# One small load on another queue, and a second norm whose instructions are tied in a written order

## The chip, the cores and the metric

The kernel runs on one core of one Trainium2 chip. The metric is the device time of one launch in microseconds (us). The kernel before was run three times: median 1348.87 us, from 1348.59 to 1349.04.

A core has five engines with one instruction queue each. PE (TensorE) multiplies matrices and takes its stationary operand through a weight load (PEld in the views). DVE (VectorE), ACT (ScalarE) and POOL (GpSimd) work elementwise. SP (SyncE) here only issues DMAs. ACT and POOL can issue DMAs as well. The transfers themselves run on 16 DMA engines.

## The reference, cut to what matters

One layer of a decoder with two request groups, 256 prompt tokens and 8 x 4 sample tokens (288 columns in the kernel), and one conditioning vector for the prompt and eight for the samples:

```python
def block(x, c, st_pool, st_conv, st_ssm, st_ffn, pos0, lp):
    mod = (silu(c) @ lp['w_ada'] + lp['b_ada'])
    sh1, sc1, g1, sh2, sc2, g2 = [m[:, None] for m in jnp.split(mod, 6, axis=-1)]
    h = rmsnorm(x, lp['norm1']) * (1 + sc1) + sh1
    proj = h @ lp['w_in']
    ...
    mix = jnp.concatenate([pool_out, ssd_out], axis=-1) @ lp['w_out']
    x = x + g1 * mix
    h2 = rmsnorm(x, lp['norm2']) * (1 + sc2) + sh2
    ffn_out, new_ffn = conv_ffn(h2, st_ffn, lp['w_up'], lp['ffn_conv_w'], lp['ffn_conv_b'], lp['w_down'])
    x = x + g2 * ffn_out
    return x, new_pool, new_conv, new_ssm, new_ffn
```

Everything is float32. The model width is 2048, which is 16 tiles of 128 (`KT`); the gated MLP has 43 tiles of 128 (`FT`).

## The kernel before, in words

**Layout and products.** Features lie on the 128 partitions, the 288 tokens on the free axis. Each weight matrix is streamed once in chunks of up to 128 x 1024 floats (512 KB). A float32 product is made of three products of a shorter format: `split` (L293) writes the rounded weight `whi` on ACT (L289) and the remainder `wlo` on DVE (L291), the operand is split into `xhi` and `xlo` in the same way (L495, L496), and `mm3` (L301) issues the three matmuls whi·xhi, whi·xlo and wlo·xhi (L303, L304, L305).

**Slots.** `load` (L267) issues a DMA on SP's queue into a slot of a ring. The class `_W` keeps the rings. Ring `raw` and ring `rawa` hold raw chunks. During the two projections before the second norm four slots are in `rawa`; L1109 moves them to `raw`, so that from there on `raw` has 12 slots and `rawa` none. There are four slots each for `whi` and `wlo` then.

**Order.** A list scheduler orders the instructions of each engine by program order, priority and readiness in its own simulation. `tc.high_priority()` lets an instruction go ahead; `in_order(...)` (L210) ties the instructions written inside it to the written order on the named engines, and leaves other instructions free to come between.

**The start.** L185 loads the conditioning vectors (`ct`, 72 KB) from SP's queue, L544 loads x in four parts (`xa`, 576 KB each) behind it, then come the first conditioning weights. ACT waits for `ct`, takes its SiLU (L208), and then squares the first part of x (L970); DVE squares the second and fourth (L972). PE sums the squares (L974).

**The conditioning product.** The six parts of `mod` are each 16 steps of k. A step is two chunks (`adap`, part, k, half) and four matmuls that stand in four column groups of PE (8 records in the trace, since each is made in two passes). Parts 0 and 1 are made by `ada_group_units`, parts 2 and 3 by `ada_visits` (L405), two steps at a time out of ring `rawa`, parts 4 and 5 by `ada_part_units` (L444), one step per call. Part 5, the gate g2, isn't needed before the down projection, so its steps serve as filling work for PE.

**The second norm.** The last output projection tile ends in `residual` (L1169, DVE) and `squares` (L1183, ACT). `final_sum` (L1199) sums the squares over partitions with PE (`col_sums`, L238, line 241), takes the root (ACT, L247) and reciprocal (DVE, L248), spreads the result over the partitions with PE into PSUM (`pb`, L254), and copies it to SBUF (ACT, L261). `modulate_steps` (L474) then makes the operand of one or two tiles: a product with rstd (L478, DVE), scale and shift of the 256 prompt columns (L486, DVE), of the 32 sample columns (L491, L492, POOL), and the split (L495 ACT, L496 DVE). The tiles k = 0 and 1 read rstd straight from PSUM, the later ones from the copy. Around it stand part 5's first five steps: two written ahead of `final_sum` and three behind it (`GA = (2, 3)`).

**The up stage.** For k = 0 to 15 the chunk `upk` (384 KB: the k-th rows of six up-projection tiles) is split and multiplied into six PSUM tiles, 18 matmuls for each k (L1244 to L1249). Two of these chunks are split ahead of the norm (L1234). Then `up_pair` (L1256) makes a gate tile and a value tile for each j; from j = 3 on two more steps of part 5 follow each pair (L1341) until all 16 are done. The down projection runs in three groups, each behind the pairs of its group.

Of the kernel before, what the change touches and what calls it, by code (L numbers as in the profile page):

```python
# [12 lines left out]
F32 = mybir.dt.float32  # L13
# [5 lines left out]
P = 128  # L19
D = 2048  # L20
KT = D // P
# [32 lines left out]

RB1, RB2, RB3 = 1.0, 1.0, 1.0
TK = 4
GA = (2, 3)
XM = (0, 2, 5, 9)
SM0 = 10
YC = [(0, 1), (1, 1)] + [(m, 2) for m in range(2, KT, 2)]  # L60
# [5 lines left out]
FK = 3  # L66
# [98 lines left out]
def kernel(ctx: ExitStack, tc, ins, outs):  # L165
    nc = tc.nc
# [13 lines left out]
    def aux(name):  # L180
        return px.tile([P, 512], F32, tag="aux", name=name)


    ct = kp.tile([P, KT, NC9], F32, tag="asb", name="ct")
    nc.sync.dma_start(ct, ins["c"])  # L185
    early = kp.tile([P, NE], F32, name="early")
    vec = kp.tile([P, NV], F32, name="vec")
    ident = early[:, K_ID:K_ID + P]
# [45 lines left out]
    def new_operand(name):  # L234
        xhi[0] = [kp.tile([P, N], F32R, tag="xhi", name=f"{name}h{k}", bufs=KT) for k in range(KT)]
        xlo[0] = [kp.tile([P, N], F32R, tag="xlo", name=f"{name}l{k}", bufs=KT) for k in range(KT)]

    def col_sums(ps, src, rhs, first, last):  # L238

        for c, a in enumerate((0, P, N - P)):  # L240
            nc.tensor.matmul(ps[:, c:c + 1], src[:, a:a + P], rhs, start=first and c == 0, stop=last,
                             skip_group_check=True)
# [24 lines left out]
    def load(key, ring="raw"):  # L267
        off, cols = S.items[key]
        t = wp[0].tile([P, RAWC], F32, tag=ring, name="raw_" + "_".join(map(str, key)))
        nc.sync.dma_start(t[:, :cols], wflat[off:off + P * cols].rearrange("(p n) -> p n", p=P))  # L270
        return t
# [21 lines left out]
    def split(raw, a, n, name, urgent=True, pin=False):  # L293
        with tc.high_priority() if urgent else nullcontext():
            cast, (hi, lo, rest) = split_steps(raw, a, n, name)
        if pin:
            tc.keep_in_program_order(cast)
            tc.keep_in_program_order(rest)
        return hi, lo
# [23 lines left out]
    def project(key, nk, opnd=None, order=None):  # L323
        for ps in project_units(key, nk, opnd, order):
            pass
        return ps


    def ada_mm(ps, raw, k, c0, nb, js):
        for j in js:  # L330
            c = c0 + (j - js[0]) * nb
            nc.tensor.matmul(ps[32 * j:32 * j + 32, :nb], sc_c[:, k, :], raw[:, c:c + nb],  # L332
                             start=(k == 0), stop=(k == KT - 1), tile_position=(0, 32 * j))
# [68 lines left out]
            nc.vector.tensor_tensor(o, src, b.unsqueeze(3).to_broadcast([P, 2, nj // 2, NC9]), ALU.add)  # L402
        ada_scale(0, 1, early[:, V_N1:V_N1 + KT], k0, gk)

    def ada_visits(parts, step):  # L405

        plan = [(part, k0) for part in parts for k0 in range(0, KT, step)]
        ahead, end = [], None

        def chunks(v):  # L410
            part, k0 = plan[v]
            for k in range(k0, k0 + step):
                for h in range(2):
                    ahead.append((k, h, load(("adap", part, k, h), "rawa")))
            yield
            yield

        yield from chunks(0)
        for v, (part, k0) in enumerate(plan):
            if end:  # L420
                ada_end(*end)
                end = None
            if k0 == 0:
                ps = pa.tile([P, 512], F32, tag="ada", name=f"adap{part}")
            n = 0
            for k, h, raw in ahead[::-1]:
                for j in (2 * h, 2 * h + 1):
                    with tc.high_priority() if n else nullcontext():
                        i = nc.tensor.matmul(ps[32 * j:32 * j + 32, :], sc_c[:, k, :],
                                             raw[:, 512 * (j % 2):512 * (j % 2) + 512], start=k == step - 1,  # L430
                                             stop=k == KT - step, tile_position=(0, 32 * j))
                    tc.keep_in_program_order(i)
                    n += 1
            ahead.clear()
            if k0 + step == KT:
                end = part, ada_sb(ps, 512, f"p{part}")
            yield
            yield
            if v + 1 < len(plan):
                yield from chunks(v + 1)  # L440
        ada_end(*end)
        yield

    def ada_part_units(part, ay=1):  # L444
        ps = pa.tile([P, 512], F32, tag="ada", name=f"adap{part}")
        for k in range(KT):
            raws = [load(("adap", part, k, h)) for h in range(2)]
            for h in range(2):
                ada_mm(ps, raws[h], k, 0, 512, range(2 * h, 2 * h + 2))
            if k % ay == ay - 1:  # L450
                yield
        asb = ada_sb(ps, 512, f"p{part}")
        yield
        ada_end(part, asb)
        yield
# [14 lines left out]
    def modulate(*args):  # L470
        for _ in modulate_steps(*args):
            pass
# [246 lines left out]
    def drain(gen):  # L719
        for _ in gen:  # L720
            pass
# [477 lines left out]
    def final_sum(name, rname, keep=True):  # L1199
        ps = fsum.pop()  # L1200
        col_sums(ps, sq_last[0], ones[:, 0:1], False, True)
        return rstd_of(ps, D, rname, keep)
# [27 lines left out]
            drain(adas)  # L1230


    adag2 = ada_part_units(5)
    for k in range(2):  # L1234
        ready[("upk", k)] = split(load(("upk", k)), 0, 2 * FK * P, f"upk{k}")
    for _ in range(GA[0]):
        next(adag2)
    rstd2p, rstd2 = final_sum("ssum2", "rstd2")
    for _ in range(GA[1]):
        next(adag2)  # L1240
    new_operand("h2")
    up0 = [(pm.tile([P, 512], F32, tag="mm", name=f"mm_up{i}") if i < 3 else aux(f"mm_up{i}"))
           for i in range(2 * FK)]
    for k0, n in [(0, 1), (1, 1)] + [(k, 2) for k in range(2, KT, 2)]:  # L1244
        modulate(x[:, k0:k0 + n, :], rstd2 if k0 > 1 else rstd2p, 1, 3, k0, n, f"n{k0}")
        for k in range(k0, k0 + n):
            hi, lo = ready.pop(("upk", k), None) or split(load(("upk", k)), 0, 2 * FK * P, f"upk{k}")
            for i in range(2 * FK):
                mm3(up0[i][:, :N], hi, lo, i, xhi[0][k], xlo[0][k], k == 0, k == KT - 1)  # L1249

# [4 lines left out]

    def up_pair(j):  # L1256
        pg = up0[2 * j] if j < FK else project(("gate", j), KT)
        gb = ff.tile([P, NG], F32, tag="gb", name=f"gb{j}", bufs=2)
        gs = gb[:, 2 + NP:].rearrange("p (b l) -> p b l", b=NB)
        nc.gpsimd.memset(gb[:, 0:2], 0.0)  # L1260
        nc.gpsimd.tensor_copy(gs[:, :, 0:2], stf[:, j])
        nc.scalar.copy(gb[:, 2:2 + NP], pg[:, 0:NP])
        nc.scalar.copy(gs[:, :, 2:6], samp(pg[:, NP:N]))
        nc.gpsimd.tensor_copy(nff[:, j, 0:2], gb[:, NP:NP + 2])
        nc.gpsimd.tensor_copy(nff[:, j, 2:18].rearrange("p (b l) -> p b l", b=NB), gs[:, :, 4:6])
        fw = V_FW + 3 * j
        gc = ff.tile([P, NG], F32, tag="gc", name=f"gc{j}", bufs=2)
        nv = NG - 2
        nc.vector.tensor_scalar(gc[:, :nv], gb[:, 0:nv], vec[:, fw:fw + 1], vec[:, V_FB + j:V_FB + j + 1],
                                ALU.mult, ALU.add)  # L1270
        for i in (1, 2):
            nc.vector.scalar_tensor_tensor(out=gc[:, :nv], in0=gb[:, i:i + nv], scalar=vec[:, fw + i:fw + i + 1],
                                           in1=gc[:, :nv], op0=ALU.mult, op1=ALU.add)
        nc.scalar.activation(gc[:, :nv], gc[:, :nv], AF.Silu)
        pv = up0[2 * j + 1] if j < FK else project(("val", j), KT)
        act = ff.tile([P, N], F32, tag="act", name=f"act{j}", bufs=2)
        nc.vector.tensor_tensor(act[:, 0:NP], gc[:, 0:NP], pv[:, 0:NP], ALU.mult)
        gcs = gc[:, 2 + NP:].rearrange("p (b l) -> p b l", b=NB)[:, :, 0:NL]
        nc.vector.tensor_tensor(samp(act[:, NP:N]), gcs, samp(pv[:, NP:N]), ALU.mult)
        ah = ff.tile([P, N], F32R, tag="ah", name=f"ah{j}", bufs=17)  # L1280
        al = ff.tile([P, N], F32R, tag="al", name=f"al{j}", bufs=17)
        nc.scalar.copy(ah, act)  # L1282
        nc.vector.tensor_tensor(al, act, ah.bitcast(F32), ALU.subtract)
        acts[j] = (ah, al)
# [53 lines left out]
    for gi, (k0, nk) in enumerate(DGROUPS):  # L1338
        for j in range(k0, k0 + nk):
            up_pair(j)  # L1340
            if gi == 0 and j >= 3:  # L1341
                next(adag2, None)
                next(adag2, None)
            if j >= SM0:
                next(states, None)
            if gi and j == k0:
                drain(adag2)
                down(gi - 1)
# [170 lines left out]
```

## Time and profile before

| what | value |
|---|---|
| median of three runs | 1348.87 us |
| the profiled execution, its own time | 1348.87 us |
| its span (first to last instruction) | 1347.1 us |
| busy PE / DVE / ACT / POOL | 99% / 61% / 43% / 17% of the span |
| bytes moved | 323.19 MB, mean 240 GB/s |
| granted PE clock, mean | 0.997 |

The profiled execution took as long as the median of the runs, so a time read in its views can be set against the median as it is. What lies outside the span (1.8 us) is launch and end. In the timeline rows a line gives the start, the time from the first start to the last end of a merged run of equal instructions, engine, line, operation, tiles, shapes and count; square brackets give how long the engine sat idle before and what ended that. A matmul's record is longer than the time in which PE can take the next one: matmuls of 288 columns follow each other every 0.13 us, while each record lasts 0.29. A record names its tiles without numbers, so `raw_adap` is a chunk of any part.

### The profile page before, as it was taken

To read this page: it belongs to the slowest core of one execution; us is meant where nothing else is said; L and a number is where in the kernel's file an instruction comes from. 1 tells how busy PE (TensorE), PEld (TensorE's weight loads), DVE (VectorE), ACT (ScalarE), POOL (GpSimd) and SP (SyncE) were. 2 spreads that over 40 slices of the span, in tenths; PEclk is the share of its full clock that TensorE was granted. 3 is DMA by queue.
4 is the path that set the end of the run, shared out by engine and by line. 5 is a ranking of instruction groups with operands and counts; after the bars stand their busy time and mean duration, and the time that the engine had idled before them with its cause. 6 is when DMAs were issued, how large, how long until landed. Compare 5 with 4: busy or idle time off the path is not lost.

```text
span 1347.1 us, 26219 instructions
## 1 busy us (share of the span) xinstructions
PE 1330.4 (99%) x10517; PEld 1245.7 (92%) x10517; DVE 822.6 (61%) x1382; ACT 576.2 (43%) x909; POOL 224.0 (17%) x449
## 2 busy tenths in 40 slices
PE   9999999999999999999999999999999999999997
PEld 7889998786799889999999999999999999999997
DVE  5675569879755468555655545666655556566543
ACT  5343245676743335433443334443433334444442
POOL 0000012123122122110211001221210011122221
PEclk9999999999999999999999999999999999999998
DMA  9999678887798877787555556555555565566521
GB/s 372 405 408 368 230 286 305 305 330 294 253 398 333 333 299 233 267 280 247 181 184 185 164 174 190 195 192 195 180 165 169 188 195 186 188 197 197 178 78 71
DMA packets 97482, 323.19 MB, mean 240 GB/s; under 512 B 10768, under 2 KB 19920, under 8 KB 97360
## 3 DMA queue, kind: packets, MB, share of 16 engines
q1 hardware_dynamic: 93600, 310.79, 66.5%
q0 software_dynamic: 3184, 9.69, 2.0%
q8 instruction: 82, 1.34, 0.4%
q10 hardware_dynamic: 576, 1.03, 0.2%
q14 instruction: 40, 0.33, 0.1%
HBM read 309.78 MB, written 10.39 MB: 238 GB/s over the span
## 4 chain that ended last, share of the span: by engine, by line
PE 93%; DVE 2%; DMA 2%; ACT 1%; issue 1%; POOL 0%; SPq 0%; DVEq 0%; POOLq 0%; ACTq 0%
PE mm_down L304 7%; PE mm_down L303 7%; PE mm_down L305 7%; PE mm_gate L303 6%; PE mm_val L304 6%; PE mm_gate L304 6%; PE mm_gate L305 6%; PE mm_val L305 6%; PE mm_val L303 6%; PE xbc L303 5%; PE xbc L304 4%; PE xbc L305 4%; PE adag L378 2%; PE adap L332 2%; PE mm_out L303 2%; PE mm_out L304 2%
## 5 line engine op out<-in xcount | busy, mean ns | idle before, releaser
L304 PE MATMUL mm_down<-al,whi_down 128*128 128x288 f32 x688 | 202.5, 294 | 0.0
L303 PE MATMUL mm_down<-ah,whi_down 128*128 128x288 f32 x688 | 202.4, 294 | 0.0
L305 PE MATMUL mm_down<-ah,wlo_down 128*128 128x288 f32 x688 | 202.0, 294 | 0.0
L304 PE MATMUL mm_val<-h2l,whi_val 128*128 128x288 f32 x640 | 189.1, 296 | 0.0
L304 PE MATMUL mm_gate<-h2l,whi_gate 128*128 128x288 f32 x640 | 189.1, 295 | 0.0
L303 PE MATMUL mm_gate<-h2h,whi_gate 128*128 128x288 f32 x640 | 188.8, 295 | 0.0
L305 PE MATMUL mm_val<-h2h,wlo_val 128*128 128x288 f32 x640 | 188.4, 294 | 0.0
L305 PE MATMUL mm_gate<-h2h,wlo_gate 128*128 128x288 f32 x640 | 188.4, 294 | 0.0
L303 PE MATMUL mm_val<-h2h,whi_val 128*128 128x288 f32 x640 | 187.9, 294 | 0.0
L291 DVE TENSOR_TENSOR wlo_gate<-raw_gate,whi_gate 128x1024 fp32r<-128x1024 f32 x80 | 98.4, 1229 | 136.5 <-ACT whi_gate L289 136.5
L291 DVE TENSOR_TENSOR wlo_down<-raw_down,whi_down 128x1024 fp32r<-128x1024 f32 x96 | 108.0, 1125 | 116.7 <-ACT whi_down L289 116.7
L289 ACT CAST whi_down<-raw_down 128x1024 fp32r<-128x1024 f32 x96 | 92.4, 962 | 167.2 <-PE mm_down L304 119.2
L289 ACT CAST whi_gate<-raw_gate 128x1024 fp32r<-128x1024 f32 x80 | 84.1, 1051 | 159.7 <-PE mm_gate L304 77.9
L289 ACT CAST whi_val<-raw_val 128x1024 fp32r<-128x1024 f32 x80 | 84.1, 1051 | 127.4 <-issue 111.3
L303 PE MATMUL xbc<-h1h,whi_xbc 128*128 128x288 f32 x448 | 133.4, 301 | 0.8 <-ACT h1h L495 0.7
L304 PE MATMUL xbc<-h1l,whi_xbc 128*128 128x288 f32 x448 | 132.0, 296 | 0.0
L305 PE MATMUL xbc<-h1h,wlo_xbc 128*128 128x288 f32 x448 | 130.3, 296 | 0.0
L303 PEld LDWEIGHTS mm_down<-ah,whi_down 128*128 128x128 f32 x688 | 129.2, 188 | 0.0
L304 PEld LDWEIGHTS mm_down<-al,whi_down 128*128 128x128 f32 x688 | 129.1, 188 | 0.0
L305 PEld LDWEIGHTS mm_down<-ah,wlo_down 128*128 128x128 f32 x688 | 129.0, 187 | 0.0
L303 PEld LDWEIGHTS mm_gate<-h2h,whi_gate 128*128 128x128 f32 x640 | 120.3, 188 | 5.0 <-ACT ah L1282 3.4
L305 PEld LDWEIGHTS mm_gate<-h2h,wlo_gate 128*128 128x128 f32 x640 | 120.5, 188 | 0.0
(334 smaller groups left out, 2978.2 us busy)
## 6 DMA issues: line engine op xcount, KB each, us to landing
raw_adap<-wflat SPq DMA_DIRECT2D x128, 512.0 KB, 5.9
raw_gate<-wflat SPq DMA_DIRECT2D x80, 512.0 KB, 3.7
raw_val<-wflat SPq DMA_DIRECT2D x80, 512.0 KB, 3.5
raw_ada<-wflat SPq DMA_DIRECT2D x64, 512.0 KB, 9.6
raw_xbc<-wflat SPq DMA_DIRECT2D x50, 512.0 KB, 9.1
raw_down<-wflat SPq DMA_DIRECT2D x48, 512.0 KB, 3.5
raw_out<-wflat SPq DMA_DIRECT2D x32, 512.0 KB, 7.3
raw_down<-wflat SPq DMA_DIRECT2D x32, 384.0 KB, 3.5
```

Of the source, the lines that this page charges most:

```text
L289: yield nc.scalar.copy(hi[:, :n], raw[:, a:a + n])
L291: yield hi, lo, nc.vector.tensor_tensor(lo[:, :n], raw[:, a:a + n], hi[:, :n].bitcast(F32), ALU.subtract)
L303: nc.tensor.matmul(ps, whi[:, w], bh, start=first, stop=False)
L304: nc.tensor.matmul(ps, whi[:, w], bl, start=False, stop=False)
L305: nc.tensor.matmul(ps, wlo[:, w], bh, start=False, stop=last)
L332: nc.tensor.matmul(ps[32 * j:32 * j + 32, :nb], sc_c[:, k, :], raw[:, c:c + nb], start=(k == 0), stop=(k == KT - 1), tile_position=(0, 32 ...
L378: i = nc.tensor.matmul(ps[32 * j:32 * j + 32, :nb], sc_c[:, ck, :], raw[:, c:c + nb], start=q0 + n == 0, stop=q0 + AQ[gi] >= nq and n + 1 ...
```

## The change

It has three parts.

1. `ct` is loaded by a DMA issued on ACT's queue; x is then the first load on SP's.
2. The second norm is written inside one `in_order` block for PE, ACT and DVE: step 0 of part 5, the column sums, the root, step 1 of part 5 between the reciprocal and the spreading matmuls (`mid`), then steps 2 and 3. Behind them stand the modulation of tiles 0 and 1, interleaved; tile 0's sample columns are made on DVE and not on POOL. The copy of rstd from PSUM (`later=True`) is written behind the reads of tiles 0 and 1 from PSUM. The split of `upk` 2 stands at the end of the block, and the split of `upk` 3 loses its high priority; it and the later ones stand behind the modulation of their tile. Four steps of part 5 are in the block, not five.
3. The other twelve steps of part 5 are made by `ada_visits`, in visits of two steps out of ring `rawa`: four slots go from `raw` to `rawa` behind the norm and stay there, so `raw` has 8 slots for the rest of the kernel. From pair 3 on, a visit's four loads are written between the gate tile and the value tile and its matmuls behind the pair. `ada_visits` takes a PSUM tile that already holds the first steps (`ps`, `begun`).

```diff
-GA = (2, 3)
+GA = 4
...
-    nc.sync.dma_start(ct, ins["c"])
+    nc.scalar.dma_start(ct, ins["c"])
...
-    def ada_visits(parts, step):
+    def ada_visits(parts, step, ps=None, begun=0):
 
-        plan = [(part, k0) for part in parts for k0 in range(0, KT, step)]
+        plan = [(part, k0) for part in parts for k0 in range(begun, KT, step)]
...
-                                             raw[:, 512 * (j % 2):512 * (j % 2) + 512], start=k == step - 1,
+                                             raw[:, 512 * (j % 2):512 * (j % 2) + 512],
+                                             start=not begun and k == step - 1,
...
-    adag2 = ada_part_units(5)
     for k in range(2):
         ready[("upk", k)] = split(load(("upk", k)), 0, 2 * FK * P, f"upk{k}")
-    for _ in range(GA[0]):
-        next(adag2)
-    rstd2p, rstd2 = final_sum("ssum2", "rstd2")
-    for _ in range(GA[1]):
-        next(adag2)
+    fill = [[load(("adap", 5, k, h)) for h in range(2)] for k in range(GA)]
+    ps5 = pa.tile([P, 512], F32, tag="ada", name="adap5")
+
+    def fill_in(k):
+        for h in range(2):
+            ada_mm(ps5, fill[k][h], k, 0, 512, range(2 * h, 2 * h + 2))
+
     new_operand("h2")
+
+    def upk(k):
+        return split(load(("upk", k)), 0, 2 * FK * P, f"upk{k}", urgent=k > 3)
+
+    with in_order(nc.tensor.engine, nc.scalar.engine, nc.vector.engine):
+        fill_in(0)
+        ssum2 = fsum.pop()
+        col_sums(ssum2, sq_last[0], ones[:, 0:1], False, True)
+        rstd2p, rstd2 = rstd_of(ssum2, D, "rstd2", mid=lambda: fill_in(1), later=True)
+        for k in range(2, GA):
+            fill_in(k)
+        mod = [modulate_steps(x[:, k:k + 1, :], rstd2p, 1, 3, k, 1, f"n{k}", None if k else nc.vector)
+               for k in range(2)]
+        for k in (0, 0, 1, 0, 1):
+            next(mod[k], None)
+        rstd2 = rstd2()
+        drain(mod[1])
+        ready[("upk", 2)] = upk(2)
+    wp[0].move("rawa", "raw", "rawa")
+    adag2 = ada_visits((5,), AK, ps5, GA)
...
     for k0, n in [(0, 1), (1, 1)] + [(k, 2) for k in range(2, KT, 2)]:
-        modulate(x[:, k0:k0 + n, :], rstd2 if k0 > 1 else rstd2p, 1, 3, k0, n, f"n{k0}")
+        if n > 1:
+            modulate(x[:, k0:k0 + n, :], rstd2, 1, 3, k0, n, f"n{k0}")
         for k in range(k0, k0 + n):
-            hi, lo = ready.pop(("upk", k), None) or split(load(("upk", k)), 0, 2 * FK * P, f"upk{k}")
+            hi, lo = ready.pop(("upk", k), None) or upk(k)
...
         pg = up0[2 * j] if j < FK else project(("gate", j), KT)
+        if j >= FK:
+            next(adag2, None)
+            next(adag2, None)
...
-            if gi == 0 and j >= 3:
+            if FK <= j:
                 next(adag2, None)
                 next(adag2, None)
```

## The prediction

> **What bounds the kernel now.** I read the page first, its busy part; then PE's waits over the whole run; then the timeline of the three places that the change touches: the start, the second norm (484 to 500 us), the up stage.
>
> ```profile
> PE 1330.4 (99%) x10517; PEld 1245.7 (92%) x10517; DVE 822.6 (61%) x1382; ACT 576.2 (43%) x909; POOL 224.0 (17%) x449
> PE adap L429 <- DMA raw_adap<-wflat: 1.1, 1, 1.1
> PE mm_up L304 <- DVE h2l L496: 0.4, 1, 0.4
> PE mm_up L303 <- ACT h2h L495: 0.4, 1, 0.4
> ```
>
> PE is busy for 99% of the span, so whatever the change brings can only come out of the few places where PE waits or is filled with work that stands there to hide a wait. The last three rows (us in total, times, longest) say how little waits openly: at the second norm 0.8 us. The rest of the norm's latency is covered by steps of part 5, which PE has to do somewhere anyway. Hidden latency is worth nothing, and a filling step taken out has to be paid where it goes.
>
> **Part 1, the start.**
>
> ```profile
> 0.74 0.39 SPq L185 DMA_DIRECT2D ct<-c  x1
> 1.19 2.12 SPq L544 DMA_DIRECT2D xa<-x  x4
> ...
> 5.79 1.15 ACT L970 ACTIVATE sq<-xa 128x1152 f32<-128x1152 f32 x1
> 8.62 1.16 ACT L970 ACTIVATE sq<-xa 128x1152 f32<-128x1152 f32 x1 [1.68 <-DMA xa<-x]
> 10.09 1.36 DVE L972 TENSOR_TENSOR sq<-xa 128x1152 f32<-128x1152 f32 x1 [1.62 <-DMA xa<-x]
> 15.15 0.38 PEld L378 LDWEIGHTS adag<-raw_ada,sc_c 128*32 128x32 f32 x16 [0.24 <-DMA raw_ada<-wflat]
> ...
> 4.00:5.00 1.00, 1.00 (x6) 1.00 (x6) 0.00 (x0) 0.97 (x3) 0.00 (x0) 1.00 1.00 406
> ```
>
> The squares of the later parts of x start when their DMA lands, and the last conditioning chunk is waited for too. The last row is a stretch of the windows view (DMA share 1.00, 406 GB/s): from 4 us on the DMA engines are full. So the start runs at the pace of the transfers behind x's first issue. That issue moves from 1.19 to 0.74: **0.45 us** earlier, for all that follows, if nothing else is in the way. In the way can be `ct` itself. Today it goes ahead of x in one queue; then it shares the DMA engines with x's first part. In the worst case it lands only when that part does: 576 KB at 406 GB/s are 1.45 us later. ACT would then square the first part that much later; but before its second square it sits idle for 1.68 us, 1.23 when x comes 0.45 earlier, so 0.22 of the 1.45 is left over. PE's sums, which stand in a row behind these squares, may add a few tenths. Bounds -0.45 and +0.2; I take -0.35, near the first, since `ct` has only an eighth of one part's bytes. Nothing else waits on ACT's queue there: its first work needs `ct`.
>
> The Trainium skill (DMA: Bandwidth & Descriptors, Queues, rings and completion order) says that each DMA engine goes round robin between the queues it has work for, a whole packet at a time; another section of that page adds that a second issuing engine saves only issue time. That speaks for the delay of `ct`; with the worst case above the term would be about -0.2 in place of -0.35. No row of before has two queues competing at the start.
>
> **Part 2, the second norm.**
>
> ```profile
> 488.44 1.92 PE L332 MATMUL adap<-raw_adap,sc_c 128*32 128x512 f32 x16
> 489.12 0.54 ACT L1186 ACTIVATE sqa<-x 128x256 f32<-128x256 f32 x2 [6.13 <-DVE rs L1173]
> 490.29 0.83 PE L241 MATMUL ssum<-ones,sqa 128*128 128x1 f32 x6
> 491.16 0.26 ACT L247 ACTIVATE r3rstd<-ssum,epst 128x3 f32<-128x3 f32 x1 [1.50 <-PE ssum L241]
> 491.45 0.18 DVE L248 RECIPROCAL r3rstd<-r3rstd 128x3 f32<-128x3 f32 x1 [2.10 <-ACT r3rstd L247]
> 492.03 0.85 PE L254 MATMUL pbrstd<-early,r3rstd 128*128 128x128 f32 x6
> 492.81 2.77 PE L332 MATMUL adap<-raw_adap,sc_c 128*32 128x512 f32 x22
> 492.92 0.40 ACT L261 COPY rstd<-pbrstd 128x288 f32<-128x288 f32 x1 [1.50 <-PE pbrstd L254]
> 493.35 0.82 DVE L478 TENSOR_TENSOR h_n<-x,pbrstd 128x288 f32<-128x288 f32 x2 [1.72 <-ACT rstd L261]
> 494.09 0.95 DVE L291 TENSOR_TENSOR wlo_upk<-raw_upk,whi_upk 128x768 fp32r<-128x768 f32 x1
> 494.96 0.73 DVE L486 TENSOR_SCALAR h_n<-h_n,amul,ada 128x256 f32<-128x256 f32 x2
> 495.45 0.43 ACT L495 CAST h2h<-h_n 128x288 fp32r<-128x288 f32 x1 [0.67 <-DVE h_n L486]
> 495.94 1.06 PE L303 MATMUL mm_up<-h2h,whi_upk 128*128 128x288 f32 x6 [0.35 <-ACT h2h L495]
> 496.98 0.40 PE L304 MATMUL mm_up<-h2l,whi_upk 128*128 128x288 f32 x1
> 498.68 0.29 PE L303 MATMUL mm_up<-h2h,whi_upk 128*128 128x288 f32 x1
> ```
>
> The reader should see three detours. The squares end at 489.66 (489.12 + 0.54), but PE is still in two filling steps (16 records) until 490.29. DVE starts the product with rstd only when ACT's copy of the same PSUM tile ends (493.35, released by it). And a weight remainder (0.95) stands on DVE between that product and the scaling. After the change, step by step:
>
> - One step ahead of the sums: 488.44 to 489.44 (a single step takes 1.00, rows under part 3). The sums start when the squares are there, **489.7** and not 490.29; PE idles 0.26, since the tie lets no other step go ahead.
> - Sums to root 0.87 (490.29 to 491.16), root to reciprocal 0.29: the reciprocal ends at 491.05. On PE the sums take 0.76 until the next instruction, then one step of 1.00: 491.46. Here PE comes last, and the spreading starts at **491.5** and not 492.03.
> - From the spreading to DVE. The tail of the kernel has the same pair without a copy in between:
>
> ```profile
> 1336.88 0.85 PE L254 MATMUL pbrstdf<-early,r3rstdf 128*128 128x128 f32 x6
> ...
> 1337.77 5.92 DVE L1371 TENSOR_TENSOR x<-xf,pbrstdf 128x288 f32<-128x288 f32 x16 [0.95 <-PE pbrstdf L254]
> ```
>
> - That is 0.89, against 1.32 at the second norm: DVE starts at 492.4. Product 0.45, scaling 0.33 until the next, then the two sample instructions, which the first norm has on DVE already:
>
> ```profile
> 17.40 0.19 DVE L491 TENSOR_TENSOR h_g<-h_g,amul 128x32 f32<-128x32 f32 x1
> ...
> 17.63 0.19 DVE L492 TENSOR_TENSOR h_g<-h_g,ada 128x32 f32<-128x32 f32 x1
> ```
>
> - 0.23 and 0.19. The operand of tile 0 is ready for ACT at about 493.65, and PE follows the cast's start by 0.49 (495.45 to 495.94): **494.2**. PE's filling ends at the same time: 491.5 + 0.78 + 1.86 for two steps = 494.15. So filling and chain are balanced, and the gain here is 1.75.
> - The remainder of tile 0 (DVE, under half a us behind the cast) is there before PE has made its first six products, so the second wait (496.98) goes. Tile 1's products start 18 x 0.131 + 0.1 = 2.46 behind tile 0's, at 496.65, and not at 498.68: **-2.0** in all. Bounds: if POOL, which still makes tile 1's samples, or an untied instruction comes between, the second half of it is lost (-1.2); if the sums start with the first of the two squares, -2.3.
>
> What is late next is DVE at **tile 2**.
>
> ```profile
> 499.89 0.77 ACT L495 CAST h2h<-h_n 128x288 fp32r<-128x288 f32 x2 [0.26 <-POOL h_n L492]
> 501.12 0.93 DVE L496 TENSOR_TENSOR h2l<-h_n,h2h 128x288 fp32r<-128x288 f32 x2
> ```
>
> Today tile 2's remainder is ready at about 501.6, and PE wants it 0.8 behind 498.68 + 2.36, at 501.84: a margin of some 0.25. Then PE wants it 2.0 earlier, at 499.8. DVE begins 0.95 earlier, but has the 0.42 for the samples more, and the remainder of `upk` 2, which used to be made during the norm (one of the two at 494.09 and behind), now comes within this stretch; the one of `upk` 3 may follow tile 2. Added up from the rows above: products 0.82, scalings 0.73, samples 0.42, remainders of operands 0.93, `upk` 2 0.95, then for tiles 2 and 3 product 0.82, scalings 0.73 and one remainder 0.45: 5.85, so 498.25 without idling. That leaves 1.55 for what DVE waits for ACT and POOL. If the product for tiles 2 and 3 falls behind the `upk` 2 remainder, which itself waits for ACT's two casts, PE stands for about 1.2. Bounds 0 and +1.2; I take +0.2, near zero, since that product needs only the copy of rstd and DVE has a hole while it waits for tile 1's cast.
>
> **Part 3, the moved step and the visits.**
>
> ```profile
> 606.66 0.29 PE L305 MATMUL mm_val<-h2h,wlo_val 128*128 128x288 f32 x1
> 606.88 1.92 PE L332 MATMUL adap<-raw_adap,sc_c 128*32 128x512 f32 x16
> 608.74 0.40 PE L303 MATMUL mm_gate<-h2h,whi_gate 128*128 128x288 f32 x1
> ...
> 621.41 0.29 PE L305 MATMUL mm_val<-h2h,wlo_val 128*128 128x288 f32 x1
> 621.63 1.06 PE L332 MATMUL adap<-raw_adap,sc_c 128*32 128x512 f32 x8
> 622.63 0.40 PE L303 MATMUL mm_gate<-h2h,whi_gate 128*128 128x288 f32 x1
> ```
>
> Two steps behind a pair cost PE 1.86 (606.88 to 608.74), one step 1.00. Today eleven steps stand there, in five twos and a single; then twelve, in six twos. The number of switches between the two kinds of matmul stays six, so the fifth step costs 1.86 - 1.00 = **+0.86** (bounds 0.8 and 1.2).
>
> The loads are as many as before. A pair with a visit takes 14.75 us (606.66 to 621.41) and asks for 8 chunks, 4.2 MB: 284 GB/s, as today and under the 406 above. `raw` has 8 slots for the rest of the kernel, and PE eats one chunk in 3.15 us (24 matmuls), so they reach 25 us ahead. I cost this at 0; the cover is that lead. Upper bound 1.1, the wait that the first visit of parts 2 and 3 had (first fence); here the first visit's slots are free from the norm on.
>
> **The sum.** -0.35 - 2.0 + 0.2 + 0.86 = -1.3. Against 1348.87, both the profiled execution and the median: **1347.6 us**. With the bounds of its terms the forecast reaches from 1346.8 to 1348.4.
>
> **The rivals.**
>
> 1. Tile 2 starves PE (above): 1347.6 + 1.0 = **1348.6**. For it: the margin of 0.25 today, with two remainders made ahead. Against it: the hole on DVE. Chance 0.16.
> 2. The start gives nothing, because `ct` comes late beside x: 1347.6 + 0.35 = **1347.95**. Chance 0.10. Against it: the idle 1.68 on ACT.
> 3. **SP blocks, slower.** A visit's four loads need all four `rawa` slots, which come free only with the last matmul of the visit before. SP's queue is in order: chunks of the value tile written behind these loads would wait too.
>
> ```profile
> 207.55 1.75 SPq L270 DMA_DIRECT2D raw_adap<-wflat  x4
> 209.35 6.55 SPq L270 DMA_DIRECT2D raw_xbc<-wflat  x3
> ```
>
>    This is how the earlier visits look: four loads in a row, and another load right behind them. If the value chunk is the fifth, 2.6 MB have to move from the visit's end on, 6.5 us at 406 GB/s, behind 1.75 for issuing the four; then its cast, about 1 us. PE wants it after a gate tile, 6.3 us. That is 2.95 us in each of five pairs: 1347.6 + 14.8 = **1362.4**. It decides as soon as value chunks are issued less than about 9.3 us ahead. Against it: in those earlier visits, with fewer slots in `raw`, PE waited once, for 1.1. Chance 0.14.
> 4. The change doesn't do what it says: the list scheduler orders untied work anew, and the tied chain gains only the first 0.6 at the sums: -0.35 - 0.6 + 0.86, **1348.8**. Chance 0.09.
>
> **How the numbers follow.** The forecast has 0.51. About 0.2% (2.7 us) is what a measurement of this kernel tells from no change; forecast and rivals 1, 2 and 4 lie inside it. Slower by more is rival 3 and a remainder for an unforeseen wait in the up stage: 0.19. Faster by more needs 1.4 beyond the forecast, more than all the terms' ends give: 0.11. Within: 0.70. The range leaves out rival 3 and the tails: 1346.3 to 1349.7.
>
> **What would show it.** Right: first issue of x near 0.74 and the last square near 9.65; sums near 489.3 and first up matmul near 493.8 (the start's 0.35 taken off); the copy of rstd behind both products; twelve steps in six visits behind pairs 3 to 8. Wrong: PE waiting for h2h or h2l at tiles 2 to 4, for `raw_val` behind a visit, or a first square on ACT later than 7.0.

## The result, and the profile after

| kernel | median | from, to | runs |
|---|---|---|---|
| before | 1348.72 us | 1348.25, 1349.30 | 18 |
| after | 1351.16 us | 1350.14, 1352.07 | 18 |

The ratio is 1.0018, with an interval from 1.0011 to 1.0025. The changed kernel is 2.4 us slower: it lies above the range, and on the other side of no change than the forecast. The profiled execution of after took 1351.21 us, so its views can be set against the median.

The page's busy part of after:

```profile
PE 1331.6 (99%) x10517; PEld 1246.4 (92%) x10517; DVE 825.5 (61%) x1384; ACT 575.8 (43%) x909; POOL 221.3 (16%) x447
```

PE has the same 10517 instructions and is busy 1.2 us longer in a span that is 2.3 longer, so in sum about half of the loss is slower work and the other half waiting. DVE has the two sample instructions more, POOL two less.

Where it went is read first from landmarks. The tile views of after give, for each product, the first and the last start of a matmul (the two numbers ahead of the semicolon):

```profile
L303 PE MATMUL xbc<-h1h,whi_xbc x448: 289/294/402, 23.0 to 256.5; 128*128 128x288 f32 x150
L305 PE MATMUL mm_outp<-mixh,wlo_out x64: 289/294/297, 378.5 to 492.1; 128*128 128x288 f32 x64
L303 PE MATMUL mm_up<-h2h,whi_upk x96: 289/295/398, 497.9 to 536.2; 128*128 128x288 f32 x96
L303 PE MATMUL mm_gate<-h2h,whi_gate x640: 289/294/402, 536.6 to 1239.4; 128*128 128x288 f32 x160
L303 PE MATMUL mm_down<-ah,whi_down x688: 292/293/380, 715.1 to 1336.0; 128*128 128x288 f32 x172
```

Set against the same landmarks of before, in hundredths as the timelines of both have them:

| landmark | before | after | lag of after | gained or lost since the landmark above |
|---|---|---|---|---|
| first xbc matmul (end of the start) | 18.58 | 22.97 | +4.39 | +4.39 |
| last output projection matmul | 488.21 | 492.10 | +3.89 | -0.50 |
| first up matmul (end of the norm) | 495.94 | 497.88 | +1.94 | -1.95 |
| first gate matmul (end of the up stage) | 535.08 | 536.63 | +1.55 | -0.39 |
| last down matmul | 1333.62 | 1335.95 | +2.33 | +0.78 |

Everything behind the start is near the prediction's terms or better (-2.0 for the norm, +0.2 for tile 2, +0.86 for the moved step). The start costs 4.4 us where a gain of 0.35 was forecast. The timeline of after shows it:

```profile
0.74 0.41 ACTq L185 DMA_DIRECT2D ct<-c  x1
0.74 2.08 SPq L545 DMA_DIRECT2D xa<-x  x4
...
5.53 1.28 ACT L208 ACT_TABLE_LOAD   x1 [5.53 <-DMA ct<-c]
...
6.73 1.36 DVE L973 TENSOR_TENSOR sq<-xa 128x1152 f32<-128x1152 f32 x1 [5.02 <-DMA xa<-x]
6.82 0.34 ACT L208 ACTIVATE sc_c<-ct 128x144 f32<-128x144 f32 x1
7.18 1.28 ACT L965 ACT_TABLE_LOAD   x1
...
8.58 1.15 ACT L971 ACTIVATE sq<-xa 128x1152 f32<-128x1152 f32 x1
9.78 1.19 PE L975 MATMUL ssum<-sq,ones 128*32 128x288 f32 x8 [3.41 <-ACT sq L971]
...
12.05 1.19 PE L975 MATMUL ssum<-sq,ones 128*32 128x288 f32 x8
...
12.21 1.16 ACT L971 ACTIVATE sq<-xa 128x1152 f32<-128x1152 f32 x1 [2.48 <-issue]
14.44 1.36 DVE L973 TENSOR_TENSOR sq<-xa 128x1152 f32<-128x1152 f32 x1 [6.34 <-PE warm L229]
```

`ct` lands 4.7 us after its issue, as late as x's first part, and ACT stands until 5.53. Behind it come a table load, the SiLU of `ct`, another table load (L965, a dummy root), and only then the first square, at 8.58 and not at 5.79. PE, which sums the squares in order, waits 3.41 us for it. Then its sums take 1.19 us each. The windows view of after shows them at half the clock (columns: window, its length, busy time and records of PE, PEld, DVE, ACT, POOL, then the granted PE clock, DMA share, GB/s):

```profile
8.00:10.00 2.00, 0.22 (x4) 0.20 (x8) 0.09 (x1) 1.72 (x3) 0.00 (x0) 0.63 1.02 420
10.00:12.00 2.00, 2.00 (x12) 0.93 (x4) 0.00 (x0) 0.00 (x0) 0.00 (x0) 0.50 1.02 410
12.00:14.00 2.00, 2.00 (x13) 1.03 (x12) 0.00 (x0) 1.16 (x1) 0.00 (x0) 0.50 1.02 399
14.00:16.00 2.00, 2.00 (x14) 0.83 (x13) 1.36 (x1) 0.00 (x0) 0.00 (x0) 0.66 1.06 384
16.00:18.00 2.00, 2.00 (x31) 1.14 (x29) 0.46 (x1) 0.00 (x0) 0.00 (x0) 1.00 1.03 405
```

The granted clock falls to 0.50 while PE waits and is back only in the window from 14 us. Cut into quarters of a microsecond, the same view puts the fall at 8.53, 2.15 us after the last matmul record of PE has ended (6.38), and the rise at 15.36: 6.83 us, the last 5.6 of them with PE at work. While PE is slow, squares three and four (12.21 and 14.44) are late too: DVE's was released by PE's `warm` matmuls, which read the squares' buffer. The transfers aren't held up: 384 to 420 GB/s throughout.

The second norm in after's timeline:

```profile
492.33 1.07 PE L332 MATMUL adap<-raw_adap,sc_c 128*32 128x512 f32 x8
...
493.48 0.83 PE L241 MATMUL ssum<-ones,sqa 128*128 128x1 f32 x6
...
495.24 0.85 PE L254 MATMUL pbrstd<-early,r3rstd 128*128 128x128 f32 x6
...
496.13 0.45 DVE L479 TENSOR_TENSOR h_n<-x,pbrstd 128x288 f32<-128x288 f32 x1 [1.31 <-PE pbrstd L254]
...
497.81 0.40 ACT L260 COPY rstd<-pbrstd 128x288 f32<-128x288 f32 x1
...
497.88 0.66 PE L303 MATMUL mm_up<-h2h,whi_upk 128*128 128x288 f32 x3
498.41 0.40 PE L304 MATMUL mm_up<-h2l,whi_upk 128*128 128x288 f32 x1
```

Counted from the last output projection matmul (488.21 before, 492.10 after), the sums start at 1.38 (2.08 before), the spreading at 3.14 (3.82), DVE's first product at 4.03 (5.14) and the first up matmul at 5.78 (7.73). The copy of rstd stands behind both products, and no second wait follows.

### The profile page after: what moved, and what is told of

Read it like the earlier page. It is cut to its first block, busy times and chain, and to the rows that moved or that the text cites. A ratio compares the mean times of both kernels' runs of the same rounds, so it can differ in the third digit from the quotient of the medians.

```text
span 1349.4 us, 26215 instructions
## 1 busy us (share of the span) xinstructions
PE 1331.6 (99%) x10517; PEld 1246.4 (92%) x10517; DVE 825.5 (61%) x1384; ACT 575.8 (43%) x909; POOL 221.3 (16%) x447
## 4 chain that ended last, share of the span: by engine, by line
PE 94%; DVE 2%; ACT 1%; issue 1%; DMA 1%; POOL 0%; DVEq 0%; SPq 0%; POOLq 0%; ACTq 0%
PE mm_down L304 7%; PE mm_down L303 7%; PE mm_down L305 7%; PE mm_gate L303 6%; PE mm_val L304 6%; PE mm_gate L304 6%; PE mm_val L305 6%; PE mm_gate L305 6%; PE mm_val L303 6%; PE xbc L303 5%; PE xbc L304 4%; PE xbc L305 4%; PE adap L429 3%; PE adag L378 2%; PE mm_out L303 2%; PE mm_out L304 2%
```

## The experiments

Each kernel is told as a change to after, or to the run named.

**e1: only the queue of `ct` put back.** Theory A: the loss is all in `ct`'s place. The rival: the new norm and the visits cost something as well.

```diff
-    nc.scalar.dma_start(ct, ins["c"])
+    nc.sync.dma_start(ct, ins["c"])
```

> The changed kernel with the load of ct back on SP's queue ahead of x; all else as changed. Theory A (the loss sits in the start alone: the first xbc matmul moved from 18.57 to 22.96 us): the start falls back to 18.6, the norm and the visits keep what they gained, and the time is 1351.2 - 4.4 = 1346.8 us, at most 1347.4. Rival B (the later parts cost something that the trace hides): 1348.7 or more.

Measured: 1346.90 us, ratio to before 0.9988 (0.9979 to 0.9996). From e1's timeline:

```profile
0.75 0.38 SPq L185 DMA_DIRECT2D ct<-c  x1
...
1.18 2.01 SPq L545 DMA_DIRECT2D xa<-x  x4
...
2.61 1.28 ACT L208 ACT_TABLE_LOAD   x1 [2.61 <-DMA ct<-c]
...
5.66 1.15 ACT L971 ACTIVATE sq<-xa 128x1152 f32<-128x1152 f32 x1
...
6.85 1.36 DVE L973 TENSOR_TENSOR sq<-xa 128x1152 f32<-128x1152 f32 x1 [5.14 <-DMA xa<-x]
```

The first xbc matmul is at 18.3, and the norm's offsets are those of after (first up matmul at 5.78). One line takes 4.3 us out of the median (4.1 when after and e1 are each set against their own runs of before). So parts 2 and 3 of the change are worth -1.7 together, with an interval of the ratio that stays just below 1, and part 1 turns that into a loss.

**e2: before, with only `ct` on ACT's queue.** The same line of the diff, on its own.

> The kernel before with one edit: ct is loaded from ACT's queue. Theory A: ct lands near 5.4 us, ACT's first square starts near 8.6, PE sits idle for over 3 us and runs at a granted clock of 0.5 for some us; first xbc matmul near 23.0, time 1348.7 + 4.4 = 1353.1 us (1352.4 if the stretch before the output projection gives 0.6 back as it did in the changed kernel). Rival B: about 1348.7.

Measured: 1352.80 us, ratio 1.0030 (1.0018 to 1.0042); first xbc matmul at 22.3. `ct` releases ACT at 5.63, PE waits 2.94 for the first square, and the granted clock is 0.50 from 9.72 to 13.13 us, cut as finely as above. The line alone costs 4.2 us against before, as much as in the changed kernel.

**e3: PE kept busy until the square comes.** The loss can be ACT's lateness or PE's clock. More dummy matmuls ahead of the sums keep PE busy, and `ct` stays late.

```diff
-WU = (14, 2, 2, 2, 6)
+WU = (26, 2, 2, 2, 6)
```

> The changed kernel with 26 in place of 14 of the idle matmuls on ones that PE makes while it waits for the first square, so PE is busy until about 10.8 us. It parts the late ct from the clock. If the clock falls because PE sat idle: the granted clock stays at 1.0, the column sums of squares take 0.7 per group and not 1.2, the first xbc matmul comes at about 20.5, time about 1348.8 us (lateness alone costs some 1.9 of the 4.4). If the clock falls for another reason: clock 0.5 again and 1351.2 us.

Measured: 1349.62 us, ratio to before 1.0009 (1.0000 to 1.0018). From e3's timeline, and its windows view:

```profile
9.87 0.69 PE L975 MATMUL ssum<-sq,ones 128*32 128x288 f32 x8 [1.09 <-ACT sq L971]
```

```profile
10.00:12.00 2.00, 2.00 (x22) 0.95 (x19) 0.00 (x0) 0.71 (x1) 0.00 (x0) 1.00 1.02 408
```

The dummies end at 8.77, sooner than the 10.8 expected, so a wait is left: it shrinks to 1.09 us. The clock stays at 1.00, a sum takes 0.69 us and not 1.19. The first square is as late as in after (8.67), the first xbc matmul comes at 20.8. That splits the start: 20.8 - 18.3 (e1) = 2.5 us for lateness, 23.0 - 20.8 = 2.2 us for the clock. Of the 2.2 the median shows only 1.5 (1351.16 - 1349.62); e3's one wait for a conditioning chunk later on (`adap` at L429) was 1.6 us, against 0.8 in after.

**e6: ACT squares first.** `ct` stays on ACT's queue, but nothing ahead of the first square needs it any more: a dummy square on `epst` brings in the table early, the SiLU of `ct` follows the first square, and the dummy root the second.

```diff
-    nc.scalar.activation(sc_c[:, :, 0:NC9], ct, AF.Silu)
+    nc.scalar.activation(warm, epst, AF.Square)
...
-        nc.scalar.activation(warm, sc_c[:, 0, 0:1], AF.Sqrt, scale=0.0)
...
+                if q == 0:
+                    nc.scalar.activation(sc_c[:, :, 0:NC9], ct, AF.Silu)
+                else:
+                    nc.scalar.activation(warm, sc_c[:, 0, 0:1], AF.Sqrt, scale=0.0)
```

> The changed kernel, ct still on ACT's queue, but ACT squares the first part of x before it takes the SiLU of ct (a one-element square ahead brings its table in early; the root's table comes after the second square). If the only harm is that ACT waits for ct: the first square starts when x's first part lands (5.2 to 5.5), PE keeps its clock, the start is 0.45 earlier than with ct ahead of x, first xbc matmul at 18.1 to 18.6, time 1346.4 to 1346.9 us. If x's parts are slowed by ct's packets too: no better than the run with ct ahead of x on SP.

Measured: 1346.65 us, ratio 0.9984 (0.9975 to 0.9993): faster than before and after, and not to be told from e1. From e6's timeline:

```profile
0.74 2.02 SPq L545 DMA_DIRECT2D xa<-x  x4
...
5.33 1.16 ACT L970 ACTIVATE sq<-xa 128x1152 f32<-128x1152 f32 x1 [2.65 <-DMA xa<-x]
...
6.78 1.36 DVE L976 TENSOR_TENSOR sq<-xa 128x1152 f32<-128x1152 f32 x1 [5.07 <-DMA xa<-x]
```

Here x is first on SP, as the change wanted, and nothing stands in its way. It is issued at 0.74, which is 0.44 ahead of e1's 1.18, yet its second part is squared at 6.78 against 6.85: 0.07 earlier. That is one execution of each. In the five traces with `ct` ahead of x on SP (before, e1, and e8 to e10 below) this square starts between 6.85 and 7.11, so the gain is 0.07 to 0.33, and not all of the hoped 0.45.

**e4: x's first part as four transfers.** Why does 72 KB take as long as 576 KB? If the engines shared by bytes, `ct` would be through early. If they take turns row by row, it is through when as many rows of its neighbour are. Here the first part has four DMAs with rows of a quarter of the size.

```diff
-        nc.sync.dma_start(t, ins["x"][:, 4 * q:4 * q + 4, :])
+        for r in range(4 if q == 0 else 1):
+            r0, n = (r, 1) if q == 0 else (0, 4)
+            nc.sync.dma_start(t[:, r0:r0 + n, :], ins["x"][:, 4 * q + r0:4 * q + r0 + n, :])
```

> The changed kernel, but x's first part is loaded in four DMAs of one tile each (rows of 1152 bytes in place of 4608). It is run for the landing of ct alone (5.4 us in the changed kernel, 4.7 behind its issue); x comes later by the three more issues, so the time isn't compared. If the DMA engines take turns between the two queues row by row, ct's rows then stand behind rows a quarter as long: ct lands near 3.5 us. If they take turns in larger portions, or ACT's queue is slow by itself: 5 us or more.

Measured: `ct` lands 3.0 us after its issue, not 4.7. One run, 1348.77 us, too few to compare. The landing alone would also come out so if an engine finished its share of the whole first transfer, here a quarter as large, before it turned to `ct`; the packets below decide between the two.

**e5, e5b, e5c: `ct` on ACT's queue with nothing beside it.** Is ACT's queue slow in itself? x's first DMA is made to wait for the SiLU of `ct`, by a copy of one element into its buffer.

```diff
+        if q == 0:
+            nc.scalar.copy(t[:, 0, 0:1], sc_c[:, 0, 0:1])
```

> The changed kernel, but x's first DMA waits for ACT's SiLU of ct (ACT writes one element of that tile first), so ct travels alone on ACT's queue. Run for the landing of ct alone; the start is late by design. If ct was late only because x travels beside it: it lands near 2.6 us, as on SP's queue ahead of x. If ACT's queue is slow by itself: near 5.4.

This didn't isolate it: three conditioning chunks moved into the empty place on SP's queue, at 0.74, and `ct` landed in 3.8 us beside them. e5b made the first conditioning chunks and the `early` vectors wait too, of which the first:

```diff
+        if key[0] in ("ada", "xbc") and key[1] == 0:
+            nc.scalar.copy(t[:, 0:1], sc_c[:, 0, 0:1])
```

> As the run before in which x's first DMA waited, but now every early load on SP's queue waits for ACT's SiLU of ct (ACT writes one element of each of those tiles first), so nothing at all travels beside ct; in that earlier run conditioning chunks had moved up into x's place. Run for the landing of ct alone. If only what travels beside it made it late: 2.6 us. If ACT's queue is slow by itself: 3.8 us or more.

Then later chunks moved up, again 3.8 us. e5c made all the early loads wait (`key[1] < 3`, and the vectors):

> Once more ct alone: now x's parts stand first on SP's queue and wait for ACT's SiLU of ct, and all early loads wait likewise (in the second try later conditioning chunks had still moved up to 0.74 us, and ct landed at 4.58). Run for the landing of ct alone. If ACT's queue is as quick as SP's: 2.6 us. If it is slow by itself: 3.5 or more, and the part of the delay that depends on what travels beside ct is smaller than thought.

Now SP's first issue was x, at 4.60, and `ct` landed in 1.9 us: ACT's queue is as fast as SP's. The three took 1352.80, 1357.83 and 1357.49 us, since all loads start late; nothing is read from these times. The row of `ct` in the DMA views of after, e4, e5 and e5c (count, KB, us to landing):

```profile
q10 hardware_dynamic: 144, 0.07, 6.7%
...
ct<-c ACTq DMA_DIRECT2D x1, 72.0 KB, 4.7
```

```profile
ct<-c ACTq DMA_DIRECT2D x1, 72.0 KB, 3.0
```

```profile
ct<-c ACTq DMA_DIRECT2D x1, 72.0 KB, 3.8
```

```profile
ct<-c ACTq DMA_DIRECT2D x1, 72.0 KB, 1.9
```

| beside `ct` | rows of the neighbour | first transfer of the neighbour lands | `ct` lands |
|---|---|---|---|
| nothing (e5c) | | | 1.9 us |
| x's first part in four (e4) | 1152 B | 2.8 us | 3.0 us |
| conditioning chunks (e5) | 4096 B | 3.6 us | 3.8 us |
| x's first part (after) | 4608 B | 4.6 us | 4.7 us |

`ct` lands 0.1 to 0.2 us behind the first transfer beside it, each time. The first row above (ACT's queue: packets, MB, share) says that `ct`'s 0.07 MB are 144 packets; it has 128 rows of 576 B, and x's part 128 rows of 4608 B. The start of every packet is kept in the traces, and shows the turns. Alone (e5c), the commonest distance between the starts of two rows of `ct` is 0.026 us. Beside the others it is 0.200 (after, where a row of x mostly takes 0.178), 0.181 (e5, a row of the chunk 0.159) and 0.073 (e4, a row 0.051): each time the neighbour's row and 0.022. So one row of `ct` goes behind each row of the neighbour, and two transfers of as many rows end together, whatever their bytes. The Trainium skill (DMA: Bandwidth & Descriptors, Queues, rings and completion order) has the turns, "at *packet* granularity", and the traces agree; it gives a packet typically some 9 to 17 descriptors, while the turns measured here are of one row.

**e8, e9, e10: the steps of the norm, one at a time, on top of e1.** e8 lets ACT copy rstd ahead of DVE's products:

```diff
-        rstd2p, rstd2 = rstd_of(ssum2, D, "rstd2", mid=lambda: fill_in(1), later=True)
+        rstd2p, rstd2 = rstd_of(ssum2, D, "rstd2", mid=lambda: fill_in(1))
...
-        rstd2 = rstd2()
```

> The run with ct on SP and the new norm, but ACT copies rstd to SBUF ahead of DVE's two products, as in the kernel before (line 1260 in place of the later copy). If the order of the two readers of that PSUM tile is worth what the two traces show (1.32 against 0.89 us from the spreading to DVE): the first up matmul comes 0.4 later, 1346.9 + 0.4 = 1347.3 us. If the copy isn't what DVE waited for: 1346.9.

e9 puts two filling steps ahead of the sums and one behind the spreading:

```diff
+        fill_in(1)
...
-        rstd2p, rstd2 = rstd_of(ssum2, D, "rstd2", mid=lambda: fill_in(1), later=True)
-        for k in range(2, GA):
+        rstd2p, rstd2 = rstd_of(ssum2, D, "rstd2", mid=lambda: fill_in(2), later=True)
+        for k in range(3, GA):
```

> The run with ct on SP and the new norm, but two of part 5's steps stand ahead of the column sums, one between reciprocal and spreading, one behind. If PE's filling is what held the sums: they start 0.6 later (2.08 behind the last output matmul in place of 1.38), and the first up matmul too or a little less, 1347.4 us. If the filling ahead costs nothing: 1346.9.

e10 puts the split of `upk` 2 between tile 0's product and its scaling:

```diff
-        for k in (0, 0, 1, 0, 1):
+        for i, k in enumerate((0, 0, 1, 0, 1)):
             next(mod[k], None)
+            if i == 0:
+                ready[("upk", 2)] = upk(2)
...
-        ready[("upk", 2)] = upk(2)
```

> The run with ct on SP and the new norm, but the split of upk 2 is tied between the first product with rstd and the scaling of tile 0, where the kernel before had a split. If a weight remainder on DVE inside the chain costs its length: first up matmul 0.8 later, 1346.9 + 0.8 = 1347.7 us, less up to 0.2 because DVE is freer at tile 2. If it lies beside PE's filling: 1346.9.

Offsets are again from the last output projection matmul:

| run | first up matmul | first gate matmul | median, against before |
|---|---|---|---|
| e1 | 5.78 | 44.6 | -1.66 |
| e8, copy first | 6.20 | 44.9 | -1.36 |
| e9, two steps ahead | 6.47 | 45.2 | -0.94 |
| e10, split inside | 7.27 | 45.6 | -0.45 |
| before, all three detours and one step more | 7.73 | 46.9 | 0 |

The ratios to before are 0.9990 (0.9981 to 1.0000) in e8, 0.9993 (0.9983 to 1.0003) in e9, 0.9996 (0.9987 to 1.0006) in e10. The medians can't separate neighbours in this table; the offsets do. The three medians lie 0.2 to 0.6 above the expected ones; before's own was 0.15 to 0.3 higher beside them than beside e1. The rows of e8 and e10 in their timelines:

```profile
492.88 0.40 ACT L261 COPY rstd<-pbrstd 128x288 f32<-128x288 f32 x1 [1.52 <-PE pbrstd L254]
493.31 0.45 DVE L479 TENSOR_TENSOR h_n<-x,pbrstd 128x288 f32<-128x288 f32 x1 [1.74 <-ACT rstd L261]
```

```profile
492.63 0.95 DVE L291 TENSOR_TENSOR wlo_upk<-raw_upk,whi_upk 128x768 fp32r<-128x768 f32 x1
...
493.93 0.95 DVE L291 TENSOR_TENSOR wlo_upk<-raw_upk,whi_upk 128x768 fp32r<-128x768 f32 x1
...
495.50 0.81 PE L303 MATMUL mm_up<-h2h,whi_upk 128*128 128x288 f32 x4 [1.42 <-ACT h2h L496]
```

In e8 DVE is released by the copy, 0.43 behind its start, and the norm is 0.42 longer. In e9 the sums start at 2.08, as in before, and the norm is 0.69 longer. In e10 the split costs 1.49, not the expected 0.8, because a second remainder, by its order that of `upk` 3, which isn't tied, came between the two sample instructions. By the first gate matmul 0.5 of it had come back: those remainders weren't owed any more. Added up, the three lengthen the norm by 2.6, while before, which has all three, is 1.95 longer than e1: they don't simply add, and e10 has one remainder more between product and cast than before.

**e11: x from both queues, on top of e6.** Would two issuing queues bring x in earlier?

```diff
-        nc.sync.dma_start(t, ins["x"][:, 4 * q:4 * q + 4, :])
+        (nc.scalar if q % 2 else nc.sync).dma_start(t, ins["x"][:, 4 * q:4 * q + 4, :])
```

> The run with the first square ahead of the SiLU, but the second and fourth part of x are issued from ACT's queue. Moving x's first issue from 1.18 to 0.74 had brought its parts only 0.07 us earlier (9.75 against 9.82 for the last). If the slow rise of the transfer rate until 4 us comes from one queue being fed by one engine, two engines raise it sooner: last square at 9.4, 1346.3 us. If the rise is that of the DMA engines themselves: 9.75 again, and 1346.6 to 1346.9 us.

Measured: 1349.68 us, ratio 1.0008 (0.9999 to 1.0018). The second and fourth part were issued from 1.26 on, but a conditioning chunk moved up between x's parts on SP (1.18), and x's last squares came later (ACT 11.19, DVE 11.61, against 8.31 and 9.75 in e6). The first xbc matmul is at 20.6. Since the order of the loads changed, this doesn't say what two queues would do with the same order.

## Why the prediction failed, point by point

**The step that failed is part 1**, "Bounds -0.45 and +0.2; I take -0.35". It measured +4.4 against before (+4.7 against e1), by four errors in a row.

- *The size of the worst case.* It was named rightly ("in the worst case it lands only when that part does") and mis-sized: 576 KB at the full rate, "1.45 us later". The landing isn't a size over a rate. A tile view of before (least, median and most, in the row below) has x's parts landing 4.5 us after issue at the soonest, and the one of `ct` 1.9; from these rows the worst case would have been 2.6, and 2.8 was measured (5.53 against before's landing at 2.7).
- *Its likelihood.* "`ct` has only an eighth of one part's bytes" decided for the near end. The packets of after, e4 and e5 go in turns of one row, so rows count, not bytes, and the rows are as many. The worst case was the case.
- *What follows it in ACT.* Two table loads of 1.28 us and the SiLU of 0.34 stand between `ct` and the first square. Before, they ran while x was under way; that cover is gone when `ct` comes with x. The forecast set the delay against the 1.68 of idle time ahead of the *second* square; but PE needs the first. Lateness alone is 2.5 us (e3 against e1).
- *What follows it in PE.* The wait of 3.41 us came with half the granted clock for 6.8 us (the windows above). That is a cost which the forecast didn't consider at all: 2.2 us at the first xbc matmul (after against e3).

```profile
DMA to landing us min/median/max: 4.5/5.9/7.4
```

The gain meant to pay for it is there only in part: 0.07 to 0.33 in e6, not 0.45. "The start runs at the pace of the transfers behind x's first issue" was read off a window from 4 us on, where the engines are full. Ahead of it they move less, and both runs reach the full rate at the same time: windows of e1 and e6 give 131 and 158 GB/s from 2 to 3 us, 263 and 308 from 3 to 4, 415 and 410 from 4 to 5. Why the rate rises only then stays open; e11 was to tell and couldn't.

The reach given for the sum, 1346.8 to 1348.4, isn't what the bounds of its terms give. Added up they go from -1.95 (-0.45 - 2.3 + 0 + 0.8) to +2.5 (+0.2 - 1.2 + 1.2 + 1.2 + 1.1), so from 1346.9 to 1351.4. The upper end was drawn too low; that 1351.16 lies inside is no credit, since part 1 alone went 4.2 us past its bound of +0.2.

**Part 2 was right.** The sums start 1.15 behind the first filling step (1.26 forecast), the product 0.89 behind the spreading (0.89), the first up matmul 1.95 earlier than before (1.75), and the second wait is gone. That the first up matmul comes early and the first gate matmul 0.4 more (together 2.34, against 2.0 less the 0.2 charged for tile 2) is the one difference. Put back one at a time, the detours cost about what the prediction read for them: the copy 0.42 (1.32 - 0.89 = 0.43), the filling step 0.69 (0.5 to 0.6), and two remainders 1.49 (each held DVE for 0.87, 492.63 to its next instruction at 493.50).

**Tile 2 didn't starve** (rival 1; +0.2 was charged). PE's waits in after list no `mm_up` row:

```profile
PE ssum L975 <- ACT sq L971: 3.4, 1, 3.4
...
PE adap L429 <- DMA raw_adap<-wflat: 0.8, 1, 0.8
```

DVE made the product for tiles 2 and 3 at 498.61, ahead of the remainder of `upk` 2 at 499.98: the hole that the prediction named.

**The moved step** was +0.86; the stretch from the first gate to the last down matmul is 0.78 longer, in e1 0.79. **SP doesn't block** (rival 3). SP's rows around a visit of after:

```profile
548.61 0.33 SPq L270 DMA_DIRECT2D raw_val<-wflat  x1
550.50 1.81 SPq L270 DMA_DIRECT2D raw_adap<-wflat  x4
552.41 0.86 SPq L270 DMA_DIRECT2D raw_val<-wflat  x1
```

A value chunk does come behind the four, but 0.1 us behind, and PE never waits for `raw_val`.

**Rival 2** ("the start gives nothing, because `ct` comes late beside x", 1347.95, chance 0.10) had the place and the mechanism, and ended on the wrong side: it took no gain for the worst, where two table loads and a clock hung on that wait. The sign given for it, "a first square on ACT later than 7.0", is what came.

The 0.5 us that after gains between the first xbc matmul and the end of the output projections wasn't forecast. PE's waits there shrank by 0.7 in sum: before's three rows `adap` 1.1, `cb` 0.8 and `y` 0.2 are 0.8 and 0.6, and `y` isn't listed. A PE that is 4.4 us late may find more of its operands there, but that is not shown: e2, 3.7 us late, gains only 0.1 in this stretch, e3, 2.2 late, loses 0.4, and e8, as early as before, loses 0.7. The 0.5 is no more than these runs differ by.

## What to carry to other kernels

Before a small load is moved off a queue where it went first, look at what hangs on it (table loads, a chain of one engine, the clock of another) and take the worst case from a landing row of the neighbour, not from its bytes over the peak rate: beside another queue's transfer of as many rows it lands when that does. Price a new wait of the bottleneck engine not only with its length but with the clock afterwards. A change of several parts can hide a good one behind a bad one: with one line put back, this one is 1.7 us faster than before.

## What the runs showed of the hardware

- A load of 72 KB issued at the same time as one of 576 KB on another queue landed in 4.7 us, alone in 1.9. The packets of the two queues went in turns of one row, so its 128 rows were through when 128 rows of the neighbour were; with neighbours' rows of 1152, 4096 and 4608 B it landed in 3.0, 3.8 and 4.7 us.
- Waits of PE of 3.41 us (after) and 2.94 (e2) came with a halved granted clock, waits of 1.09 (e3) and 1.86 (e11) didn't. The fall came 2.15 us (after) and 2.78 (e2) behind the end of PE's last record, and the clock stayed at 0.50 for 6.83 us in after and 3.41 in e2, so a wait half a microsecond longer went with twice the time at half speed. The Trainium skill (TensorE: Matmul & The Clock Gate, Part 1: The HAM clock gate) puts both the idle time that lowers the clock and the busy time that restores it at a window of about 3.4 us which runs free of the kernel. The 3.41 and twice 3.41 agree with such windows; that PE must idle for 3.4 us doesn't agree, 2.15 sufficed.
- A table load in ACT's queue waits for the operand of the instruction behind it (5.53, released by `ct`). With a dummy instruction that needs no such operand (e6) it ran at 1.19, ahead of the wait.
